# Fill products behind the state product, heads in turn, and a read in four parts in a two-layer hybrid mixer

## The chip, the core and the metric
The program runs on one core of one Trainium2 chip. Time is the device time of one execution in microseconds (us). The engines are named as in the profile: PE is TensorE (PEld its weight loads), DVE VectorE, ACT ScalarE, POOL GpSimd, SP SyncE, which issues the DMAs here.

## What is computed
Two layers on 512 tokens of width 1024, all in float32. Each layer is a SwiGLU block, a mixer with three branches, and a second SwiGLU block, each added to the stream behind an RMS norm. The branches are a retention (8 heads, chunks of 128 tokens), an attention over the 256 keys that an index score selects, and RWKV-7. The change lies in RWKV-7 and in the retention. RWKV-7 is, per head of 64, a recurrence over the tokens:

```
def step(S, inp):
    r_t, w_t, k_t, v_t, kk_t, a_t = inp
    sa = jnp.einsum('bhvk,bhk->bhv', S, -kk_t)
    S = S * w_t[:, :, None, :] + sa[..., None] * (kk_t * a_t)[:, :, None, :] + v_t[..., None] * k_t[:, :, None, :]
    return S, jnp.einsum('bhvk,bhk->bhv', S, r_t)
```

The retention computes within each chunk `scores = jnp.einsum('bhid,bhjd->bhij', qc, kc) * decay_mask` and multiplies them with the values.

## The kernel before, in words
Everything lies feature by token, in tiles of 128 partitions by 512 tokens. The large products (SwiGLU, all projections, the merge) are run as three float32r products each of a high and a low part (lines 109, 111, 113, `mm3`); the split of every weight tile costs ScalarE one copy (L49) and VectorE one subtraction (L50), and its load comes by SyncE (L54) into one of four `raw` buffers.

RWKV-7 is computed in 8 chunks of 64 tokens, for two heads at a time: a head pair p = 0 to 3 fills the 128 partitions, head 0 on rows 0 to 63, head 1 on rows 64 to 127. A pair passes through four stages. `front2` makes decays, keys and stacked operands. `mid` multiplies `bk` by `st` for each chunk and head (L444, a product over 64 rows: the head's), masks the result on VectorE into `nb`, `zo` and `st` (L449 to L451), transposes some operands, and then inverts a triangular matrix for each chunk: the 32x32 blocks of `nb` go to DRAM (four DMAs, L480, tile `dn`), come back as `N`, all 32 blocks side by side and repeated four times over the partitions (L481; the trace calls this tile by the name of its buffer, bk), and POOL solves row by row in 31 steps of two instructions (L490, L492, tile X, named cum in the trace). After every fourth step a one-column product, the pace product (L494), makes TensorE wait for that step. The blocks of the inverse go to DRAM and back once more (L497, L503) and are put together (L504, L510, L517). `chain` then runs the 8 chunks one after the other: the product with the state (L533), a copy on VectorE (L536), the product with the inverse (L543), copies (L547), the state product (L553), the state update on VectorE (L556), and the output product (L558) with its sum Y (L562). L533, L543, L553 and L558 of a chunk write parts of one product buffer. `post` normalises.

Two product buffers (tag "r") serve mid, chain, front2 and post in turn; two (tag "f") serve retention and attention; four (tag "d") the dense products.

TensorE executes in one order, which a planner fixes at build time: it places instructions by level (the recurrence, "rec", first; fills, "norm", behind) as soon as its own clock has their operands ready. The other branches and the merge are a second stream of work. `K.fill(n, after)` takes n dense products from that stream, and ties them behind the instruction `after` on TensorE. The counts were written out by hand: FZ = 11 behind each group of L444, FV = 38 behind the transposes, FP = 11 to 15 behind each pace product, FD = 29 behind the last, and FC = 6, 6, 5, 6 (by head pair) three times in each chunk of the chain. `front2` of the next pair runs in steps within the chain of this one.

`Ret.heads` works on two heads as well: for each head four products over its 64 rows into one buffer (L673), then a mask on VectorE (L675). `kd` (L636, POOL) is the decayed key that L652 multiplies.

Of the kernel before, what the change touches and what calls it, by code (L numbers as in the profile page):

```python
# [7 lines left out]
P = 128  # L8
# [215 lines left out]
FZ, FV, FD, FB, FE = 11, 38, 29, 5, 46  # L224
FP = 12, 11, 11, 15
FM = 6, 0, 2, 7
FC = 6, 6, 5, 6
# [5 lines left out]
class Rwkv:  # L233
# [198 lines left out]
    def mid(self, d):  # L432

        nc, K, c = self.nc, self.K, self.cst
        st, bk, v = d["st"], d["bk"], d["v"]
        zo, nb = self.zo, self.t("kh", [P, 8, 64])
        for q in range(2):
            for h in range(2):
                s = slice(64 * h, 64 * h + 64)
                o = slice(64 - 64 * h, 128 - 64 * h)  # L440
                z = K.ps("r")
                for i in range(4):
                    ck = 4 * q + i
                    zl = nc.tensor.matmul(z[:, i * P:(i + 1) * P], bk[s, ck, :], st[h][s, ck, :], start=True, stop=True)  # L444
                K.fill(FZ, zl)
                z3 = z.rearrange("p (i t) -> p i t", i=4)
                mk = c["zmask"][:, h, None, :].to_broadcast([P, 4, P])
                cs = slice(4 * q, 4 * q + 4)
                nc.vector.tensor_tensor(out=nb[s, cs, :], in0=z3[s, :, s], in1=mk[s, :, s], op=ALU.mult)  # L449
                nc.vector.tensor_tensor(out=zo[s, cs, o], in0=z3[s, :, o], in1=mk[s, :, o], op=ALU.mult)  # L450
                nc.vector.tensor_tensor(out=st[h][o, cs, :], in0=z3[o], in1=mk[o], op=ALU.mult)  # L451
        with self.tc.issue_after(zl.ins):

            bt = d["bt"] = self.t("bkt", [P, 8, P])
            for q in range(2):
                pt = K.ps("r")
                for i in range(4):
                    K.turn(pt[:, i * P:(i + 1) * P], bk[:, 4 * q + i, :])
                nc.scalar.activation(bt[:, 4 * q:4 * q + 4, :], pt.rearrange("p (c t) -> p c t", c=4), AF.Copy)
            sv = d["sv"] = [self.t("sv0", [P, 8, 64]), self.t("sv1", [P, 8, 64])]  # L460
            pv = K.ps("r")
            for i in range(4):
                self.gate = K.turn(pv[:, i * P:(i + 1) * P], v[:, i * P:(i + 1) * P])
            pv4 = pv.rearrange("p (i h d) -> p i h d", i=4, h=2)
            for h in range(2):
                o = slice(64 - 64 * h, 128 - 64 * h)
                for par in range(2):
                    src = pv4[64 * par:64 * par + 64, :, h, :]
                    nc.scalar.activation(sv[h].rearrange("p (i e) d -> p i e d", e=2)[o, :, par, :], src, AF.Copy)
                nc.gpsimd.memset(sv[h][64 * h:64 * h + 64, 0, :], 0.0)  # L470
        if d["p"] < 3:
            K.urgent.append(self.front(d["p"] + 1, self.blk))
        K.fill(FV, self.gate)

        dn = K.dram([4, 8, 32, 32], "dn", 2)
        N = self.t("bk", [P, 32, 32])
        for h in range(2):
            for b in range(2):
                src = nb[64 * h + 32 * b:64 * h + 32 * b + 32, :, 32 * b:32 * b + 32]
                nc.sync.dma_start(dn[2 * h + b].rearrange("c s t -> s c t"), src)  # L480
        nc.sync.dma_start(N, dn.rearrange("b c s t -> (b c) s t")[None].to_broadcast([4, 32, 32, 32]))  # L481

        X = self.t("cum", [P, 8, 32])
        tmp = self.t("E", [P, 8 * 31])
        nc.sync.dma_start(X, c["idg"])
        FI, pz = FP[d["p"]], K.ps("r")
        for u in range(31):
            n, w = u // 4 + 1, 31 - u
            tv = tmp[:, :n * w].rearrange("p (s j) -> p s j", s=n)
            nc.gpsimd.tensor_tensor(out=tv, in0=X[:, 0:n, u:u + 1].to_broadcast([P, n, w]),  # L490
                                    in1=N[:, u:u + 1, u + 1:].to_broadcast([P, n, w]), op=ALU.mult)
            nc.gpsimd.tensor_tensor(out=X[:, 0:n, u + 1:], in0=X[:, 0:n, u + 1:], in1=tv, op=ALU.add)  # L492
            if FI and (u % 4 == 3 or u == 30):
                pace = nc.tensor.matmul(pz[:, u:u + 1], K.ident, X[:, 0, u + 1:u + 2], start=True, stop=True)  # L494
                K.fill(FI if u < 30 else FD, pace)
        dx = K.dram([4, 8, 32, 32], "dx", 2)
        nc.sync.dma_start(dx.rearrange("b c (i g) t -> g (b c) i t", g=4), X)  # L497
        mt = self.mt
        m1 = self.t("m1", [P, 8, 32])
        for h in range(2):  # L500
            a = 64 * h
            for b in range(2):
                nc.sync.dma_start(mt[a + 32 * b:a + 32 * b + 32, :, a + 32 * b:a + 32 * b + 32], dx[2 * h + b].rearrange("c s t -> s c t"))  # L503
            nc.vector.transpose(m1[a:a + 32].rearrange("p c t -> p (c t)"), mt[a:a + 32, :, a:a + 32])  # L504
            nc.gpsimd.memset(mt[a + 32:a + 64, :, a:a + 32], 0.0)
        pc = K.ps("r")
        cc = m1
        for a in (0, 64):
            for ck in range(8):
                mm = nc.tensor.matmul(pc[a + 32:a + 64, ck * 32:ck * 32 + 32], nb[a:a + 32, ck, 32:64], m1[a:a + 32, ck, :],  # L510
                                      start=True, stop=True)
        K.fill(2 * FB, mm)
        for a in (0, 64):
            nc.scalar.activation(cc[a + 32:a + 64], pc[a + 32:a + 64, :256].rearrange("p (c t) -> p c t", c=8), AF.Copy)
        for a in (0, 64):
            for ck in range(8):
                mm = nc.tensor.matmul(pc[a:a + 32, ck * 32:ck * 32 + 32], cc[a + 32:a + 64, ck, :], mt[a + 32:a + 64, ck, a + 32:a + 64],  # L517
                                      start=True, stop=True)
        K.fill(2 * FB, mm)
        for a in (0, 64):  # L520
            nc.scalar.activation(mt[a:a + 32, :, a + 32:a + 64], pc[a:a + 32, :256].rearrange("p (c t) -> p c t", c=8), AF.Copy)

    def chain(self, d, step):

        nc, K = self.nc, self.K
        st, bt, sv, gch = (d[x] for x in ("st", "bt", "sv", "gch"))
        Y = d["Y"] = self.t("Y", [P, 8, 64])
        half = lambda h: (slice(64 * h, 64 * h + 64), slice(64 - 64 * h, 128 - 64 * h))
        for ck in range(8):
            a = K.ps("r")  # L530
            a3 = a.rearrange("p (n h d) -> p n h d", n=4, h=2)
            for h in range(2):
                mm = nc.tensor.matmul(a3[:, 0, h, :], st[h][:, ck, :], sv[h][:, ck, :], start=True, stop=True)  # L533
# [5 lines left out]
            uvf = uv.rearrange("p h d -> p (h d)")  # L539
            for h in range(2):  # L540
                s, o = half(h)
                nc.gpsimd.tensor_copy(uv[o, h, :], sv[h][o, ck, :])
            mm = nc.tensor.matmul(a[:, 2 * P:3 * P], self.mt[:, ck, :], X, start=True, stop=True)  # L543
            K.fill(FC[d["p"]], mm)
            for h in range(2):
                s, o = half(h)
                nc.vector.tensor_copy(uv[s, h, :], a3[s, 2, h, :])  # L547
            if ck < 7:
                B = self.t("cb", [P, 64], bufs=2)
                for h in range(2):  # L550
                    s, o = half(h)
                    nc.vector.tensor_scalar(out=B[s], in0=sv[h][s, ck, :], scalar1=gch[s, ck:ck + 1], scalar2=None, op0=ALU.mult)
                nc.tensor.matmul(a[:, P:2 * P], bt[:, ck, :], uvf, start=True, stop=True)  # L553
                for h in range(2):
                    s, o = half(h)
                    nc.vector.scalar_tensor_tensor(out=sv[h][s, ck + 1, :], in0=a3[s, 1, h, :], scalar=gch[s, ck:ck + 1], in1=B[s],  # L556
                                                   op0=ALU.mult, op1=ALU.add)
            mm = nc.tensor.matmul(a[:, 3 * P:], self.zo[:, ck, :], uvf, start=True, stop=True)  # L558
            K.fill(FC[d["p"]] if ck < 7 else FE, mm)
            for h in range(2):  # L560
                s, o = half(h)
                nc.vector.tensor_tensor(out=Y[o, ck, :], in0=a3[o, 3, h, :], in1=X[o, s], op=ALU.add)  # L562
# [38 lines left out]
class Ret:  # L601
# [43 lines left out]
    def heads(self, q, X, kd):  # L645
        K, nc, c = self.K, self.nc, self.c

        pk = K.ps()
        for j in range(3):
            for h in range(2):  # L650
                s = slice(64 * h, 64 * h + 64)
# [8 lines left out]
        for o, dst in ((0, qT), (P, kT)):  # L660
            pt = K.ps()
            for t in range(4):
# [1 line left out]
            nc.scalar.activation(dst, pt, AF.Copy)  # L664
        nc.gpsimd.tensor_tensor(out=qd.rearrange("p (c i) -> p c i", c=4), in0=qT.rearrange("p (c i) -> p c i", c=4),
                                in1=self.qdec[:, None, :].to_broadcast([P, 4, P]), op=ALU.mult)
        sT = []
        for h in range(2):
            s = slice(64 * h, 64 * h + 64)
            pt = K.ps()  # L670
            for j in range(4):
                f = slice(j * P, j * P + P)
                last = nc.tensor.matmul(pt[:, f], kT[s, f], qT[s, f], start=True, stop=True)  # L673
            x = self.t("sT", bufs=2)
            nc.vector.tensor_tensor(out=x.rearrange("p (c i) -> p c i", c=4), in0=pt.rearrange("p (c i) -> p c i", c=4),  # L675
                                    in1=self.dm[:, h:h + 1, :].to_broadcast([P, 4, P]), op=ALU.mult)
            sT.append(x)
# [480 lines left out]
```

## Time and profile before

| | |
|---|---|
| median of three runs | 3042.56 us (3041.69 to 3042.8) |
| the profiled execution | 3045.66 us, of which its span 3043.9 us |
| TensorE matmuls busy | 2908.3 us (96%) |
| VectorE busy | 1741.9 us (57%) |
| ScalarE busy | 1082.4 us (36%) |
| POOL busy | 736.7 us (24%) |
| mean granted clock of TensorE | 0.982 |
| the chain that ended last | PE 73%, DVE 10%, POOL 7%, DMA 6% |

A float32 product of small tiles shows as two records (a count of x8 is four products). Matmul records overlap, so the distance from start to start tells more than their length. A wait in the list of waits is idle time of the engine, put down to what ended it.

### The profile page before, as it was taken

The page shows a single profiled execution, that of the slowest core. Times are in us where ns is not written, and L with a number is a line of the kernel's source. Part 1 is how long each engine was busy: PE and PEld are TensorE (multiplying, and loading weights), DVE is VectorE, ACT ScalarE, POOL GpSimd, SP SyncE. Part 2 cuts the span into 40 slices and gives each one's busy share as a digit, 9 for nine tenths or more (in the row PEclk, how much of TensorE's full clock was granted, in tenths as well). Part 3 has the DMA queues.
Part 4 walks back from the last instruction along what each step waited for, and adds up shares of the span by engine and source line. Part 5 has one row for each costly group of instructions (what it writes and reads, how often), then busy time and mean ns, then how long its engine had stood idle before and what let it go on. Part 6 is the DMA issues. An engine that isn't in the chain of part 4 may idle for free.

```text
span 3043.9 us, 39972 instructions
## 1 busy us (share of the span) xinstructions
PE 2908.3 (96%) x13968; PEld 2378.0 (78%) x13968; DVE 1741.9 (57%) x3694; ACT 1082.4 (36%) x1900; POOL 736.7 (24%) x1206
## 2 busy tenths in 40 slices
PE   9999999899899999999999999998988999999998
PEld 7888887777777778888888888777777777788886
DVE  5443378949674564444354433888485836644433
ACT  4333343244443233333333333533344432433322
POOL 2110124353433031110011101343534321311100
PEclk9999999999999999999999999999999999999999
DMA  4333322122324442333323334221323244423332
GB/s 137 97 97 104 112 92 73 63 88 81 94 84 148 131 153 94 97 97 95 100 94 97 97 107 118 83 71 60 95 74 97 92 143 132 145 94 97 97 97 87
DMA packets 198970, 305.66 MB, mean 100 GB/s; under 512 B 45808, under 2 KB 59888, under 8 KB 198768
## 3 DMA queue, kind: packets, MB, share of 16 engines
q1 hardware_dynamic: 198768, 303.10, 32.7%
q8 instruction: 110, 1.80, 0.3%
q14 instruction: 92, 0.75, 0.1%
HBM read 273.66 MB, written 29.36 MB: 100 GB/s over the span
## 4 chain that ended last, share of the span: by engine, by line
PE 73%; DVE 10%; POOL 7%; DMA 6%; issue 3%; ACT 1%; SPq 0%; DVEq 0%; POOLq 0%; ACTq 0%
PE psd L109 22%; PE psd L113 22%; PE psd L111 22%; POOL cum L492 3%; POOL E L490 2%; DMA bk<-dn 2%; DVE wlo L50 2%; DMA dx<-cum 1%; PE psr L444 1%; PE psr L533 1%; DMA th<-th 1%; PE psf L96 1%; DMA y<-y 1%; PE psr L558 1%; PE psr L96 1%
## 5 line engine op out<-in xcount | busy, mean ns | idle before, releaser
L49 ACT ACTIVATE whi<-raw 128x512 fp32r<-128x512 f32 (+2 forms) x920 | 571.3, 622 | 1300.8 <-PE psd L111 1002.6
L50 DVE TENSOR_TENSOR wlo<-raw,whi 128x512 fp32r<-128x512 f32 (+2 forms) x920 | 646.3, 703 | 552.7 <-ACT whi L49 545.4
L109 PE MATMUL psd<-xh,whi 128*128 128x512 f32 x2144 | 853.5, 398 | 1.5 <-DVE g L203 1.5
L111 PE MATMUL psd<-xl,whi 128*128 128x512 f32 x2144 | 848.9, 396 | 2.2 <-DVE xl L161 2.2
L113 PE MATMUL psd<-xh,wlo 128*128 128x512 f32 x2144 | 849.2, 396 | 0.1
L111 PEld LDWEIGHTS psd<-xl,whi 128*128 128x128 f32 x2144 | 408.1, 190 | 87.2 <-DVE xl L161 4.3
L113 PEld LDWEIGHTS psd<-xh,wlo 128*128 128x128 f32 x2144 | 408.0, 190 | 84.8 <-issue 0.7
L109 PEld LDWEIGHTS psd<-xh,whi 128*128 128x128 f32 x2144 | 408.5, 191 | 83.3 <-DVE g L203 1.7
L207 POOL TENSOR_TENSOR u<-s,u 128x512 f32<-128x512 f32 x88 | 140.9, 1602 | 841.6 <-DVE u L206 745.3
L109 PE MATMUL psd<-ah,whi 128*128 128x512 f32 x704 | 277.4, 394 | 0.0
L113 PE MATMUL psd<-ah,wlo 128*128 128x512 f32 x704 | 276.0, 392 | 0.0
L111 PE MATMUL psd<-al,whi 128*128 128x512 f32 x704 | 273.2, 388 | 0.0
L172 POOL TENSOR_TENSOR sq<-sq,sq 128x512 f32<-128x512 f32 x42 | 56.4, 1342 | 466.0 <-ACT sq L170 466.0
L111 PE MATMUL psd<-wlo,xh 128*128 128x512 f32 (+1 forms) x384 | 159.2, 415 | 0.0
L113 PEld LDWEIGHTS psd<-ah,wlo 128*128 128x128 f32 x704 | 132.1, 188 | 31.0
L111 PEld LDWEIGHTS psd<-al,whi 128*128 128x128 f32 x704 | 132.2, 188 | 29.6
L113 PE MATMUL psd<-whi,xl 128*128 128x512 f32 (+1 forms) x384 | 154.8, 404 | 0.0
L109 PEld LDWEIGHTS psd<-ah,whi 128*128 128x128 f32 x704 | 132.3, 188 | 26.3
L50 DVE TENSOR_TENSOR al<-u,ah 128x512 fp32r<-128x512 f32 x88 | 61.8, 702 | 153.6 <-ACT ah L49 153.6
L109 PE MATMUL psd<-whi,xh 128*128 128x512 f32 (+1 forms) x384 | 149.7, 410 | 0.0
L206 DVE TENSOR_TENSOR u<-psd,rb 128x512 f32<-128x512 f32 x88 | 60.9, 692 | 127.6 <-PE psd L113 127.6
L49 ACT ACTIVATE ah<-u 128x512 fp32r<-128x512 f32 x88 | 55.6, 632 | 169.4 <-POOL u L207 169.2
(305 smaller groups left out, 3946.6 us busy)
## 6 DMA issues: line engine op xcount, KB each, us to landing
raw<-in_wf_dram SPq DMA_DIRECT2D x184, 256.0 KB, 2.6
raw<-in_ffa_in_dram SPq DMA_DIRECT2D x176, 256.0 KB, 2.6
raw<-in_ffb_in_dram SPq DMA_DIRECT2D x176, 256.0 KB, 2.6
th<-th SPq DMA_DIRECT2D x96, 256.0 KB, 3.3
raw<-in_ffa_out_dram SPq DMA_DIRECT2D x80, 256.0 KB, 2.7
raw<-in_wt_dram SPq DMA_DIRECT2D x80, 256.0 KB, 2.8
raw<-in_ffb_out_dram SPq DMA_DIRECT2D x80, 256.0 KB, 2.6
x<-x SPq DMA_DIRECT2D x32, 256.0 KB, 4.4
```

The source lines that it names most:

```text
L49: self.nc.scalar.activation(hi, x, AF.Copy)
L50: self.nc.vector.tensor_tensor(out=lo, in0=x, in1=hi.bitcast(F32), op=ALU.subtract)
L96: return self.nc.tensor.transpose(out, x, self.ident)
L109: nc.tensor.matmul(out, ah, bh, start=start, stop=False)
L111: nc.tensor.matmul(out, ah, bl, start=False, stop=False)
L113: nc.tensor.matmul(out, al, bh, start=False, stop=stop)
L172: nc.gpsimd.tensor_tensor(out=sq, in0=sq, in1=self.ssq[0], op=ALU.add)
L206: nc.vector.tensor_tensor(out=u, in0=pu, in1=self.rb, op=ALU.mult)
L207: nc.gpsimd.tensor_tensor(out=u, in0=s, in1=u, op=ALU.mult)
L444: zl = nc.tensor.matmul(z[:, i * P:(i + 1) * P], bk[s, ck, :], st[h][s, ck, :], start=True, stop=True)
L490: nc.gpsimd.tensor_tensor(out=tv, in0=X[:, 0:n, u:u + 1].to_broadcast([P, n, w]), in1=N[:, u:u + 1, u + 1:].to_broadcast([P, n, w]), op=AL ...
L492: nc.gpsimd.tensor_tensor(out=X[:, 0:n, u + 1:], in0=X[:, 0:n, u + 1:], in1=tv, op=ALU.add)
```

## The change
Three places. In `chain` the fill that stood behind the output product L558 of the chunks 0 to 6 stands behind the state product L553; the last chunk keeps its fill FE. In `mid` the products of both heads are issued in turn into two buffers, with one fill of 2 x FZ behind both instead of FZ behind each, and then the masks of both heads; `heads` does the same with L673, without fills. In `mid` the read of `N` is issued as four DMAs of eight rows each instead of one.

```diff
         for q in range(2):
+            zz = [K.ps("r") for _ in range(2)]
+            for i in range(4):
+                ck = 4 * q + i
+                for h in range(2):
+                    s = slice(64 * h, 64 * h + 64)
+                    zl = nc.tensor.matmul(zz[h][:, i * P:(i + 1) * P], bk[s, ck, :], st[h][s, ck, :], start=True, stop=True)
+            K.fill(2 * FZ, zl)
             for h in range(2):
                 s = slice(64 * h, 64 * h + 64)
                 o = slice(64 - 64 * h, 128 - 64 * h)
-                z = K.ps("r")
-                for i in range(4):
-                    ck = 4 * q + i
-                    zl = nc.tensor.matmul(z[:, i * P:(i + 1) * P], bk[s, ck, :], st[h][s, ck, :], start=True, stop=True)
-                K.fill(FZ, zl)
-                z3 = z.rearrange("p (i t) -> p i t", i=4)
+                z3 = zz[h].rearrange("p (i t) -> p i t", i=4)
...
-        nc.sync.dma_start(N, dn.rearrange("b c s t -> (b c) s t")[None].to_broadcast([4, 32, 32, 32]))
+        for u in range(0, 32, 8):
+            src = dn.rearrange("b c s t -> (b c) s t")[:, u:u + 8, :]
+            nc.sync.dma_start(N[:, u:u + 8, :], src[None].to_broadcast([4, 32, 8, 32]))
...
-                nc.tensor.matmul(a[:, P:2 * P], bt[:, ck, :], uvf, start=True, stop=True)
+                mm = nc.tensor.matmul(a[:, P:2 * P], bt[:, ck, :], uvf, start=True, stop=True)
                 for h in range(2):
                     s, o = half(h)
                     nc.vector.scalar_tensor_tensor(out=sv[h][s, ck + 1, :], in0=a3[s, 1, h, :], scalar=gch[s, ck:ck + 1], in1=B[s],
                                                    op0=ALU.mult, op1=ALU.add)
+                K.fill(FC[d["p"]], mm)
             mm = nc.tensor.matmul(a[:, 3 * P:], self.zo[:, ck, :], uvf, start=True, stop=True)
-            K.fill(FC[d["p"]] if ck < 7 else FE, mm)
+            if ck == 7:
+                K.fill(FE, mm)
...
-        sT = []
-        for h in range(2):
-            s = slice(64 * h, 64 * h + 64)
-            pt = K.ps()
-            for j in range(4):
-                f = slice(j * P, j * P + P)
-                last = nc.tensor.matmul(pt[:, f], kT[s, f], qT[s, f], start=True, stop=True)
+        sT, ps = [], [K.ps() for _ in range(2)]
+        for j in range(4):
+            f = slice(j * P, j * P + P)
+            for h in range(2):
+                s = slice(64 * h, 64 * h + 64)
+                last = nc.tensor.matmul(ps[h][:, f], kT[s, f], qT[s, f], start=True, stop=True)
+        for h, pt in enumerate(ps):
             x = self.t("sT", bufs=2)
```

## Rows read from the trace of the kernel before

**Rows 1.** The page, busy time of each engine (us, share of the span, instructions).
```profile
PE 2908.3 (96%) x13968; PEld 2378.0 (78%) x13968; DVE 1741.9 (57%) x3694; ACT 1082.4 (36%) x1900; POOL 736.7 (24%) x1206
```

**Rows 2.** Who waited for whom, TensorE over the whole span: us in total, times, longest us.
```profile
PE psr L494 <- POOL cum L492: 24.8, 20, 5.7
PE psr L533 <- DVE sv L556: 17.8, 24, 1.8
PE psr L510 <- DVE m L504: 12.0, 14, 2.4
...
PE psf L652 <- POOL kd L636: 7.1, 4, 3.3
PE psr L553 <- DVE uv L547: 6.1, 8, 1.6
...
PE psr L558 <- DVE sv L556: 3.8, 4, 1.3
```

**Rows 3.** Timeline of TensorE in a chunk of the last head pair's chain, first layer: start, length, line, operation, tiles, shapes, count, idle time before.
```profile
1008.92 0.38 PE L553 MATMUL psr<-uv,bkt 128*128 128x128 f32 x2
1009.68 0.43 PE L533 MATMUL psr<-sv,stk 128*128 128x64 f32 x2 [0.37 <-DVE sv L556]
1010.00 0.49 PE L558 MATMUL psr<-uv,zo 128*128 128x128 f32 x2
1010.32 0.33 PE L533 MATMUL psr<-sv,stk 128*128 128x64 f32 x2
...
1010.78 0.39 PE L111 MATMUL psd<-yl,whi 128*128 128x512 f32 x1
...
1013.32 0.39 PE L543 MATMUL psr<-cx,mt 128*128 128x128 f32 x2
...
1014.95 0.38 PE L553 MATMUL psr<-uv,bkt 128*128 128x128 f32 x2
```

**Rows 4.** Timeline of VectorE in the same chunk.
```profile
1009.35 0.60 DVE L556 SCALAR_TENSOR_TENSOR sv<-psr,gch,cb 64x64 f32<-64x64 f32 x2 [0.89 <-PE psr L553]
...
1010.91 0.27 DVE L536 COPY cx<-psr 128x128 f32<-128x128 f32 x1
```

**Rows 5.** Busy time by stretch: the chains of the first, third and fourth head pair of the first layer. Columns: stretch, its length, then busy us and instructions of PE, PEld, DVE, ACT, POOL, then the granted clock, the DMA share and GB/s.
```profile
512.00:600.00 88.00, 77.86 (x444) 62.17 (x442) 82.54 (x224) 28.37 (x50) 31.98 (x50) 0.94 0.23 71
...
850.00:914.00 64.00, 57.34 (x314) 46.70 (x313) 54.05 (x155) 27.10 (x54) 25.33 (x29) 1.00 0.25 78
...
990.00:1046.00 56.00, 52.98 (x263) 43.91 (x262) 29.94 (x87) 10.76 (x17) 2.81 (x12) 1.00 0.39 123
```

**Rows 6.** Timeline of TensorE around products of 64 rows, of 64 columns and of full size, from three stretches.
```profile
447.06 0.39 PE L111 MATMUL psd<-wlo,xh 128*128 128x512 f32 x1
...
447.38 1.16 PE L444 MATMUL psr<-stk,bk 64*128 64x128 f32 x8
...
448.80 0.39 PE L109 MATMUL psd<-whi,xh 128*128 128x512 f32 x1
...
470.49 0.66 PE L652 MATMUL psf<-X,kd 128*64 128x128 f32 x8
...
498.55 0.60 PE L686 MATMUL psf<-X,sT 128*128 128x128 f32 x4
...
771.38 1.71 PE L444 MATMUL psr<-stk,bk 64*128 64x128 f32 x16
```

**Rows 7.** Timeline of TensorE, the retention's score products of one pair of heads.
```profile
491.89 1.16 PE L673 MATMUL psf<-qT,kT 64*128 64x128 f32 x10
...
493.43 0.93 PE L673 MATMUL psf<-qT,kT 64*128 64x128 f32 x6
```

**Rows 8.** Timeline of TensorE at the end of the first head pair's chain: the next pair's first L444, and this pair's last L558.
```profile
598.80 1.16 PE L444 MATMUL psr<-stk,bk 64*128 64x128 f32 x8
...
604.00 0.49 PE L558 MATMUL psr<-uv,zo 128*128 128x128 f32 x2
```

**Rows 9.** Timeline of VectorE there.
```profile
601.51 0.41 DVE L450 TENSOR_TENSOR zo<-psr,zmask 64x256 f32<-64x256 f32 x1
...
604.53 0.46 DVE L562 TENSOR_TENSOR Y<-psr,cx 64x64 f32<-64x64 f32 x2
```

**Rows 10.** Timeline of POOL, the first step of the first inversion loop.
```profile
474.72 0.24 POOL L490 TENSOR_TENSOR E<-cum,bk 128x31 f32<-128x31 f32 x1 [7.05 <-DMA bk<-dn]
```

**Rows 11.** The chain that ended last, in order of time: start, length, what.
```profile
463.96 10.62 DMA bk<-dn
```

**Rows 12.** Timeline of TensorE behind two pauses (first head pair; third head pair).
```profile
476.51 0.70 PE L652 MATMUL psf<-X,kd 128*64 128x128 f32 x4 [3.25 <-POOL kd L636]
...
477.73 0.63 PE L111 MATMUL psd<-wlo,xh 128*128 128x512 f32 x1
478.16 0.63 PE L113 MATMUL psd<-whi,xl 128*128 128x512 f32 x1
...
802.42 0.38 PE L494 MATMUL psr<-cum,ident 128*128 128x1 f32 x2 [4.69 <-POOL cum L492]
```

**Rows 13.** Busy time by stretch, a microsecond while the N of the fourth head pair is read (columns as in rows 5).
```profile
936.00:937.00 1.00, 1.00 (x6) 0.75 (x6) 0.00 (x0) 0.01 (x1) 0.00 (x0) 1.00 0.26 86
```

**Rows 14.** DMA issues: tiles, engine, count, KB each, median us from issue to landing.
```profile
cum<-in_idg_dram SPq DMA_DIRECT2D x8, 128.0 KB, 2.0
```

**Rows 15.** Line 481 by itself: count, duration of the issue on SyncE in ns (min/median/max), first and last start.
```profile
L481 SPq DMA_DIRECT2D bk<-dn x8: 541/542/678, 464.0 to 2443.8; - x8
```

## Prediction
> **What bounds the kernel now.** I read the page first: TensorE's matmuls are busy 95.5% of the span, VectorE's instructions 57% [rows 1]. The kernel is one long row of dense products, and what can be won is the time in which TensorE stands still or runs products badly packed. Second, the list of who waited for whom, TensorE alone [rows 2]: the largest entries are the three the change touches. The pace products (L494) wait 24.8 us for POOL's inversion loop, the state products (L533) 17.8 us for VectorE's state update (L556), the blocks of the inverse (L510) 12.0 us for what comes after that loop; L652 waits 7.1 us for kd (L636), which stands on POOL behind the loop's first step. Third, the timeline of one chunk of the chain [rows 3, 4]; fourth, the timelines of the 64-row products [rows 6, 7]; last, the transfer that the loop starts on [rows 10 to 15].
>
> **Part A, the third fill of the chain.** A chunk from one L553 to the next takes 1014.95 - 1008.92 = 6.03 us [rows 3]. Its work: 18 fill products at 0.23 us from start to start (the second of twelve starts at 1010.78, L543 behind the last at 1013.32: eleven steps), 4.1 us; ten records of small products at about 0.1 us, 1.0 us; together 5.1 us. So 0.9 us is lost, and the rows say where: L553 starts at 1008.92, needs 0.22 us, and the first L533 starts at 1009.68, because VectorE's L556 runs from 1009.35 to 1009.95 [rows 4]. L558 then stands between the two L533 and each waits a little (starts 0.32 us apart instead of about 0.2). Nothing is queued on TensorE that could stand in this gap, since the fill is tied behind L558, and L558 writes the product buffer that L556 reads (its own wait for L556 is 3.8 us [rows 2]). Behind the gap twelve fills follow in a row (2.8 us) where the copy of L536, which L543 needs, ends at 1011.18 [rows 4], 0.9 us after the second L533 started.
> After the change six fills (1.4 us) stand in the gap, which needs 1009.95 - 1009.14 = 0.8 us of cover; six stay before L543, which needs about 0.9 us. No fill is added or dropped. Expected loss per chunk: about 0.15 us; gain 0.75 us where VectorE is free. Chunks with a state product: 7 x 8 pairs = 56. The four head pairs of a layer differ by VectorE's load: 53% in the last one's chain, 94% in the first's and 84% in the third's [rows 5], and I take the second to lie between; there a reply of VectorE comes late whatever TensorE does, and six fills will not always cover it. The nearest row for such a reply behind six fills is L553 waiting for L547: 6.1 us in 8 waits [rows 2]. Last head pairs: 14 x 0.75 = 10 us. The others: 42 x 0.35 (about half) = 15 us. A = **25 us**. Bounds: the waits of L533 and L558 alone, 21.6, less two stretches like L553's 6.1, gives 9; all 56 at 0.75 gives 42. New waits: L558 and the Y sums (L562) come 1.4 us later and hold their product buffer that much longer; the buffer's ring has two, so this matters only while the other is taken (rival 3).
>
> **Part B, products of L444.** A batch of eight records takes from 447.06 (the fill before) to 448.80 (second fill after), 1.74 us, where two fill steps take 0.46: 1.28 us, of which eight records at 0.11 are 0.9 us and 0.4 us are the change of shape before and after [rows 6]. Whether rows 0-63 and rows 64-127 run beside each other has two rows of this trace. Two batches that happen to be neighbours take 1.71 us for 16 records, not twice 1.16 [rows 6]. And L652, which alternates halves of the columns, brings eight records in 0.66 us where four of L686 take 0.60 [rows 6]. So I take both heads in turn at the time of one batch: 1.28 us for 16 records. There are 16 such couples of batches (two a head pair). In the first head pair of each layer they stand apart (4 couples): 1.28 us each, 5 us. In the other 12 they are partly neighbours already, or the first head's batch runs inside the previous chain and its partner must wait for the second ring buffer [rows 8]; 0.25 us each, 3 us. B = **8 us**, bounds 3 and 16.
> The Trainium skill (TensorE: Matmul & The Clock Gate, Part 3) has products in strict order in start and end; by that rule neighbouring batches could not have gained anything and B would be nearer 16. The 1.71 us of this trace disagree: some of the overlap is there already.
> The 22 fills now stand in one block behind both heads, 5.1 us, where eleven (2.5 us) covered three of VectorE's instructions each time; they now cover six, and nothing is charged. If VectorE is late there, the next couple waits for both buffers.
>
> **Part D, products of L673.** Eight uses; four have a pace product in the middle (1.16 + 0.93 us) [rows 7], four are 16 neighbours. At 1.28 each they save 1 us and 0.4 us: 5.6 us if all are laid as meant; half the split ones will be split again by a pace product that has precedence. D = **4 us**, bounds 0 and 6.
>
> **Part C, four parts of N.** POOL waits 7.05 us until 474.72 [rows 10], for a transfer that took 10.6 us [rows 11], and everything behind it on POOL waits too, kd among it (TensorE idles 3.25 us for it before 476.51 [rows 12]). While it runs, the transfers keep 0.26 of 16 engines busy [rows 13], about four. A quarter has 128 KB; the load of idg, of that size, lands in 2.0 us [rows 14]. A quarter of the 10.6 less 2.0, and 2.0: about 4.2 us; so L490 can start up to 6 us earlier, if it waits for its own eight rows alone. That it can: L450 wrote chunks 0 to 3 of zo at 601.51 while L558 had yet to read chunk 7 of that tile at 604.00 [rows 8, 9], so dependencies go by region. The loop's first eight rows are two of its stretches, with 11 to 15 fills beside each (2.5 us and more), and the parts follow each other by about 2.2 us, so the later ones are hidden. SyncE issues three more transfers of 0.54 us [rows 15]; the weight loads queued behind them come 1.6 us later, which four raw buffers cover; without them a late load would cost TensorE at most that, 8 x 1.6 = 13 us.
> What the 6 us are worth: at most the waits that hang on the loop, 24.8 + 12.0 + 7.1 = 43.9 us [rows 2]. TensorE however reaches the first pace product earlier too, by B, and past some point its own queue is the bound. I take the long waits of the first pace products, such as the 4.69 us before 802.42 [rows 12], at 14 us of the 24.8, and half of L652's 7.1: C = **18 us**. Bounds: 5 (the one longest kind of wait, once in each layer) and 44.
>
> **The clock.** In the mixers the granted clock falls: its mean is 0.94 over the first chain and 1.00 over the third and fourth [rows 5]. It is 1.2 GHz in parts of the first: after the 3.25 us of idling, fills start 0.43 us apart [rows 12], not 0.23. Over the chain of 88 us 0.06 is 5 us. Idle stretches that go take some of this with them: **5 us** in all, bounds 0 and 25.
>
> **Sum.** 25 + 8 + 4 + 18 + 5 = 60 us. The profiled execution took 3045.66 us (span 3043.9, 1.8 around it), 3.1 us over the median of 3042.56. 3045.7 - 60 = 2985.7, less 3.1: **2983 us**. Under 0.2% (6 us) a measurement cannot tell a change of this kernel.
>
> **Rivals.** 1. VectorE becomes the bound of the first three chains (84 to 94% busy): A keeps the last pairs' 10 us, C half, no clock: 10 + 8 + 4 + 9 = 31 us, 3012. For it: the load [rows 5]; against it: part of that load is top-k work that has no haste.
> 2. All waits go and the clock stays up: 42 + 10 + 5 + 25 + 13 = 95 us, 2948. For it: the idle time is short and scattered, so a little cover reaches far.
> 3. Slower: the ring of two product buffers. L558 and Y late, the front work of the next pair in the other buffer, so the next L533 has to wait for Y: about 1.1 us (L558 0.2, Y 0.9) in up to 30 chunks, 33 us; and at 6 ends of chains the second head's batch waits, from 598.80 to Y's end at 604.99 [rows 8, 9], which strips TensorE of a batch and 11 fills of cover, 3.7 us each, 22 us. Against it 16 (26 free chunks at 0.6) + 3 + 4 + 18 = 41 us: 14 us slower, 3057. It decides from stalls of 41 us on. Against it: now, too, Y comes only after L533's wait, and front products leave their buffer within about a microsecond.
> 4. The four parts do not do what they should: L490 waits for the last, which is issued 1.6 us later than the one of now. C is 0 to -13 us (1.6 x 8): 3001 to 3014, I say 3003. The Trainium skill has a rule on its side: DMA: Bandwidth & Descriptors (Bandwidth) wants at least 1 MiB in a transfer, and by its fit (Anatomy of one DMA, for transfers that GpSimd issues) of 2.0 us plus the bytes over 436 GB/s a whole N would be an estimated 3.2 us and a quarter 2.3, so that C would be 7 us and the time 2994. The 10.6 us of this trace disagree with that fit.
>
> **How the numbers follow.** Forecast 0.42; rival 1 0.24; rival 2 0.14; rival 3 0.04; rival 4 0.12; no change that can be told, by gains and stalls that cancel, 0.04. Faster 0.92, same 0.04, slower 0.04. Range: 2948 to 3022: rivals 1, 2 and 4 lie in it; above it are rival 3, no change and the tail of 1.
>
> **What will show it.** A: fills between L553 and L533, and L533's wait for L556 under 8 us. B, D: 16 records in about 1.2 us. C: L490 starting 4 to 5 us after the first part's issue, L494's waits under 8 us. Wrong if L533 now waits for L562, if L543 waits for L536 by over 10 us, or if POOL still waits 10 us.

## The result, and the profile after

The changed kernel takes 3000.66 us (median of four, 3000.12 to 3009.55), the kernel before 3042.68 beside it: ratio 0.9855, 95% interval 0.9835 to 0.9876. That is 42 us less by the medians and 44 by the ratio (38 to 50), where 60 were forecast; 3000.7 lies within 2948 to 3022. The profiled execution took 3000.62 us, its span 2998.8. Its mean granted clock is 0.986, where the kernel before had 0.982; in the three other runs of the changed kernel it is 0.983.

TensorE's list of waits, by columns as in rows 2. Lines have moved: L494 is now L498, L533 L537, L510 L514, L652 L658, L553 L557, L558 L563, L543 L547, L562 L568, L444 L443, L490 L494, L673 L678.

```profile
PE psr L498 <- POOL cum L496: 14.8, 23, 1.6
PE psr L514 <- DVE m L508: 12.2, 12, 2.2
PE psf L96 <- POOL o L706: 8.6, 4, 4.2
PE psr L390 <- DVE Y L568: 8.2, 6, 1.9
...
PE psr L537 <- DVE sv L560: 5.3, 3, 2.8
...
PE psr L443 <- DVE Y L568: 5.0, 5, 2.6
...
PE psr L284 <- DVE Y L568: 3.6, 4, 1.5
```

Against [rows 2] the pace products wait 14.8 us instead of 24.8, and no longer than 1.6 at a time instead of 5.7; the products with the state (L537) 5.3 instead of 17.8; L658's 7.1 are gone from the top. The blocks of the inverse wait as before (12.2 and 12.0). Three lines tell of Y: 8.2 + 5.0 + 3.6 = 16.8 us in which TensorE, at first products of other work (L390 and L284 in the front work, L443 the 64-row products), waits for a product buffer until the Y sums have read it. In the kernel before, L284 alone had such a wait, 1.2 us.

A chunk of the last head pair's chain, first layer, TensorE and then VectorE (columns as in rows 3 and 4):

```profile
995.88 0.38 PE L557 MATMUL psr<-uv,bkt 128*128 128x128 f32 x2
996.02 0.48 PE L109 MATMUL psd<-yh,whi 128*128 128x512 f32 x1
...
997.50 0.33 PE L537 MATMUL psr<-sv,stk 128*128 128x64 f32 x2
997.66 0.44 PE L563 MATMUL psr<-uv,zo 128*128 128x128 f32 x2
997.94 0.33 PE L537 MATMUL psr<-sv,stk 128*128 128x64 f32 x2
998.08 0.48 PE L109 MATMUL psd<-yh,whi 128*128 128x512 f32 x1
...
999.56 0.38 PE L547 MATMUL psr<-cx,mt 128*128 128x128 f32 x2
...
1001.17 0.38 PE L557 MATMUL psr<-uv,bkt 128*128 128x128 f32 x2
```
```profile
996.30 0.60 DVE L560 SCALAR_TENSOR_TENSOR sv<-psr,gch,cb 64x64 f32<-64x64 f32 x2 [0.90 <-PE psr L557]
...
998.22 0.46 DVE L568 TENSOR_TENSOR Y<-psr,cx 64x64 f32<-64x64 f32 x2
998.60 0.27 DVE L540 COPY cx<-psr 128x128 f32<-128x128 f32 x1
```

It takes 1001.17 - 995.88 = 5.29 us, 0.74 less than [rows 3]. Fills stand from 996.02 on; the state update ends at 996.90, 0.6 us before L537 wants it.

The 64-row products, in two stretches (columns as in rows 6):

```profile
447.06 1.16 PE L443 MATMUL psr<-stk,bk 64*128 64x128 f32 x8
448.14 0.45 PE L759 MATMUL psf<-kih,qs 128*128 128x384 f32 x1
448.43 0.34 PE L760 MATMUL psf<-X,qs 128*128 128x384 f32 x1
448.69 1.16 PE L443 MATMUL psr<-stk,bk 64*128 64x128 f32 x8
...
612.81 1.16 PE L443 MATMUL psr<-stk,bk 64*128 64x128 f32 x16
613.90 0.50 PE L113 MATMUL psd<-whi,xl 128*128 128x512 f32 x1
```

Where the heads really alternate, 16 records take the 1.16 us of eight [rows 6]. But only 6 of the 16 couples (the two heads' batches of one stretch of four chunks) came out so. In the other ten the planner issued the first head's four products as soon as they were ready, and other work stands between the heads.

POOL's first step of the inversion, and the four reads by themselves (columns as in rows 10 and 15):

```profile
468.33 0.24 POOL L494 TENSOR_TENSOR E<-cum,bk 128x31 f32<-128x31 f32 x1 [3.28 <-DMA bk<-dn]
```
```profile
L485 SPq DMA_DIRECT2D bk<-dn x32: 499/510/725, 464.0 to 2408.1; - x32
```

The first quarter is issued at 464.0 and POOL starts at 468.33, 4.3 us later, where the whole took 10.6 us to land [rows 10, 11]. Over the eight head pairs it is 4.1 to 6.7 us, the longest in the fourth pairs; in the kernel before, 9.4 to 12.0.

### The profile page after: what moved, and what is told of

The parts are those of the page before. It is cut to its first block, busy times and chain, and to the rows that moved or that the text cites. A ratio compares the mean times of both kernels' runs of the same rounds, so it can differ in the third digit from the quotient of the medians.

```text
span 2998.8 us, 39997 instructions
## 1 busy us (share of the span) xinstructions
PE 2884.7 (96%) x13968; PEld 2356.4 (79%) x13968; DVE 1751.9 (58%) x3694; ACT 1081.0 (36%) x1900; POOL 739.9 (25%) x1206
```

## The experiments

All are timed beside the kernel before. First each part alone: a_only, b_only, c_only and d_only hold the diff's hunk for `chain`, for L444, for the read of N and for L673, and nothing else.

**a_only.**
```diff
+                K.fill(FC[d["p"]], mm)
...
-            K.fill(FC[d["p"]] if ck < 7 else FE, mm)
+            if ck == 7:
+                K.fill(FE, mm)
```


> The kernel before with part A alone (third fill behind the state product). As predicted, A is worth 25 us: 3018 us. The theory that A works only in the last head pair's chain, where VectorE is half idle and no front work of a next pair uses the product buffers, expects its two chains to be 5 us shorter each and the other six unchanged within 3 us: about 3030 us, and waits of front products for Y in the list of waits, as in the changed kernel (16 us there).

Measured 3036.42 us, 0.9976 (0.9966 to 0.9986): 7 us, not 25. TensorE's waits:

```profile
PE psr L494 <- POOL cum L492: 25.3, 16, 5.2
PE psr L510 <- DVE m L504: 16.5, 14, 2.3
PE psr L96 <- DVE bc L396: 15.5, 4, 5.5
PE psf L654 <- POOL kd L638: 12.9, 4, 3.8
```

The 17.8 us of L533 are gone from the top, so A does its work; others have grown. The eight chains, each from the start of its first L533 to that of its last L558, sum to 581.7 us (590.8 before), the mids in front of them, from the first 64-row product on, to 643.3 (634.6): of 9.1 us won 8.7 are given back there. The last pairs' chains are 5.6 us shorter each, as the second theory says, and its waits for Y are there (7.7 + 3.7 + 2.9 us); the time is 6 us over its 3030. What is given back lies in the mids of the fourth head pairs, 7.2 and 4.3 us longer (the other six together 2.8 shorter), and only there does the read of N land more than a microsecond later. In the first layer POOL starts 13.5 us after the issue at 933.38, where before it took 9.3 (933.47 to 942.81), in the second 14.0 instead of 10.2:

```profile
946.87 0.24 POOL L490 TENSOR_TENSOR E<-cum,bk 128x31 f32<-128x31 f32 x1 [9.36 <-DMA bk<-dn]
```

Busy time by stretch while N is read, the kernel before and then a_only (columns as in rows 5; the DMA share is the last but one):

```profile
936.00:938.00 2.00, 2.00 (x12) 1.66 (x12) 0.82 (x2) 0.96 (x2) 0.00 (x0) 1.00 0.37 113
938.00:940.00 2.00, 2.00 (x11) 1.61 (x10) 0.47 (x1) 1.71 (x5) 0.00 (x0) 1.00 0.62 176
```
```profile
936.00:938.00 2.00, 2.00 (x12) 1.67 (x10) 1.22 (x2) 1.88 (x6) 0.57 (x2) 1.00 1.02 253
938.00:940.00 2.00, 2.00 (x10) 1.65 (x9) 0.37 (x1) 1.17 (x3) 0.00 (x0) 1.00 1.06 217
...
944.00:946.00 2.00, 0.99 (x5) 0.49 (x3) 0.00 (x0) 0.00 (x0) 0.00 (x0) 1.00 0.63 157
946.00:948.00 2.00, 0.00 (x0) 0.00 (x0) 0.00 (x0) 0.00 (x0) 1.03 (x5) 0.79 0.40 155
```

Other transfers fill the DMA engines (share 1.0 instead of 0.4 to 0.6) while N crosses, and TensorE, out of covering work, stands from 945 to 948. In the second layer the share is 0.83 over the read. That the other transfers make N late is read from these shares, not tested by itself. The clock has a part as well: over the twelve runs of a_only its mean is 0.978, over the kernel before's beside them 0.982.

**b_only** (the hunk for L444, with the fill of 2 x FZ).

> The kernel before with part B alone (64-row products of mid, both heads in turn, one fill of 22 behind them). As predicted 8 us: 3035 us, most of it in the first head pair of each layer. The theory that B's worth is mostly in the earlier start of the inversion (eleven fills fewer ahead of the last product) expects more, 3025 to 3030 us, with the pace products' waits for POOL below 20 us instead of 24.8. The theory that the second product buffer is missed at the ends of the chains expects 3040 us or more.

Measured 3045.59 us, 1.001 (0.9999 to 1.0021): nothing, or up to 0.2% lost. That is the time of the third theory, but waits of the 64-row products for Y, which it implies, are not in the list.

**c_only** (the read of N in four DMAs).

> The kernel before with part C alone (N read in four parts). As predicted 18 us: 3025 us, the first step of the loop 4 to 7 us behind the first issue instead of 10.6, the pace products' waits under 12 us, the blocks' wait (L510) unchanged near 12 us. If the page rule against small transfers were right, 7 us: 3036 us. If what is gained ahead of the loop is given back behind it, 3035 us or more, with L510 waiting over 16 us.

Measured 3023.37 us, 0.9931 (0.9917 to 0.9945): 21 us. TensorE's waits:

```profile
PE psr L535 <- DVE sv L558: 22.4, 24, 3.3
...
PE psr L496 <- POOL cum L494: 8.8, 14, 1.1
```

The pace products wait 8.8 us instead of 24.8, and POOL's first step comes 3.8 to 5.3 us after the first issue in all eight head pairs. The products with the state (here L535) wait 22.4 us; in b_only and d_only it is 23.8 and 25.0, so that the growth from 17.8 is not C's alone.

**d_only** (both heads in turn in L673).

> The kernel before with part D alone (the retention's score products, both heads in turn). As predicted 4 us: 3039 us. The rival, that the planner's new order costs what the overlap saves, expects 3041 to 3045 us, and the score products' batches still cut by pace products.

Measured 3043.54 us, 0.9996 (0.9985 to 1.0007): no difference. Four of the eight uses are 16 records in 1.16 us, the other four are still cut by a pace product.

**ac**: both together, without B and D.

> The kernel before with parts A and C. Alone they measured ratios of 0.9976 and 0.9931, together by multiplication 0.9907 (3014 us); the whole change has 0.9855. Theory that what A wins in the chains is given back at the inversion's read of N and is kept only where C shortens that read: 3000 to 3006 us (ratio 0.986 to 0.988). Theory that the missing part is B's doing: 3012 to 3016 us.

Measured 3001.31 us, 0.9849 (0.9833 to 0.9865): the whole change. Against c_only, A on top of C is 0.9849/0.9931 = 0.9917, 25 us (19 to 32 by the two intervals); alone it was 7. The chains by head pair, c_only and ac, both layers:

| head pair | 1 | 2 | 3 | 4 |
|---|---|---|---|---|
| c_only, us | 95.8, 94.9 | 82.0, 82.0 | 67.3, 67.5 | 57.6, 57.6 |
| ac, us | 97.4, 96.6 | 81.5, 76.1 | 65.4, 63.4 | 50.5, 50.6 |

The chains are 23 us shorter: 14.1 in the last pairs, 6.0 in the third, 6.4 in the second, and 3.3 longer in the first. But a length also counts the fills and front products that the planner put into the chain. The last pair's, first layer, c_only and then ac (columns as in rows 5):

```profile
978.10:1036.00 57.90, 54.88 (x270) 45.48 (x269) 30.90 (x89) 12.01 (x19) 2.85 (x12) 1.00 0.39 120
```
```profile
975.00:1025.80 50.80, 50.80 (x261) 42.81 (x260) 29.77 (x87) 10.76 (x17) 3.20 (x12) 1.00 0.43 135
```

c_only's chain has nine products more, 2.1 us at 0.23 us each; the other 5.0 us are A's. Counted in this way in all eight chains (an estimate, with 0.23 us for a product of 512 columns and 0.11 for a record of a small one), A brings 10 us in the last pairs, 7 in the third, and in the second and first nothing that can be told: 18 us. What is left of the 25 lies outside the chains.

**bc**: B and C.

> The kernel before with parts B and C. By multiplication 0.9941 (3025 us). Theory that the read of N hides what A wins: 3022 to 3027 us, B adds nothing here. Theory that B's tighter products pay once the loop no longer holds TensorE up: 3010 to 3015 us.

Measured 3024.1 us, 0.9925 (0.991 to 0.994), with C alone 0.9931: B brings nothing with the wait for N out of the way either.

**tied**: the whole change, and each 64-row product tied behind the one before, so that one head's products can't run ahead of the other's; head 1 now comes first.
```diff
+            zl = None
             for i in range(4):
                 ck = 4 * q + i
-                for h in range(2):
+                for h in (1, 0):
                     s = slice(64 * h, 64 * h + 64)
-                    zl = nc.tensor.matmul(...)
+                    with ExitStack() as es:
+                        if zl:
+                            es.enter_context(self.tc.issue_after(zl.ins))
+                        zl = nc.tensor.matmul(...)
```


> The whole change, with each 64-row product of the mids tied behind the one before it, heads in turn, so that the two heads' products come alternately wherever both buffers are there. In the changed kernel 10 of the 16 couples still stood apart as two batches of eight. Theory 1 (B gave nothing because the order of the build split the couples): ten couples at 1.28 us less each than two batches, up to 10 us: 2988 to 2995 us, and batches of 14 to 16 records. Theory 2 (a batch's price is not on the path, because the time is made up at the next wait for VectorE or POOL or for the second product buffer): 2997 to 3004 us. Theory 3 (the first head's products now wait for the second head's buffer, and TensorE with them): over 3004 us.

Measured 3009.8 us, 0.9892 (0.9878 to 0.9906): 11 us slower than the changed kernel by the ratios. TensorE at the first couple of the second head pair, L447 being the 64-row products:

```profile
604.39 0.48 PE L447 MATMUL psr<-stk,bk 64*128 64x128 f32 x2
...
610.01 1.16 PE L447 MATMUL psr<-stk,bk 64*128 64x128 f32 x14
```

In 12 of the 16 couples the planner still splits off one product, and the other seven follow as 14 records in 1.16 us; the first pairs' four couples come whole. But here the 14 come at 610 us, and the masks run on VectorE from 612.9. In the changed kernel the first head's eight come at 602.1, inside the previous chain, and its masks run from 604.03. From a chain's end to the next pair's first pace product, in the first layer, it is now 31.9, 33.4 and 31.9 us instead of 22.7, 26.1 and 27.2. Only the first pair, whose couples were split with both buffers free, reaches it sooner (26.9 us from its first 64-row product instead of 29.3). Part of that is work moved: the eight chains are 36 us shorter in all, as the early batch and its fills no longer stand in them. So theory 1 falls: the couples packed cost 11 us more, and theory 3 fits the place. That the early half batch was worth more than the packing is argued from these times; the tie also cut six couples that had been whole.

**zofirst**: the output product ahead of the state product in the chunks 0 to 6, the fill behind both.
```diff
             if ck < 7:
                 ...
+                nc.tensor.matmul(a[:, 3 * P:], self.zo[:, ck, :], uvf, start=True, stop=True)
                 mm = nc.tensor.matmul(a[:, P:2 * P], bt[:, ck, :], uvf, start=True, stop=True)
                 ...
                 K.fill(FC[d["p"]], mm)
-            mm = nc.tensor.matmul(a[:, 3 * P:], self.zo[:, ck, :], uvf, start=True, stop=True)
             if ck == 7:
+                mm = nc.tensor.matmul(a[:, 3 * P:], self.zo[:, ck, :], uvf, start=True, stop=True)
                 K.fill(FE, mm)
```


> The changed kernel with the output product ahead of the state product in chunks 0 to 6, the fill behind both. Ring theory (Y comes late behind the fill, holds one of two product buffers, and front products and 64-row products wait for it, 16.8 us in the changed kernel): these waits for Y fall under 5 us, the chains of the first three head pairs shorten by 2 to 4 us each, 2985 to 2993 us. VectorE theory (84 to 94% busy in those chains): waits move to other instructions, time within 4 us of the changed kernel. Price: the state product comes 0.22 us later in 56 chunks, behind six fills that cover it.

Measured 2996.64 us, 0.9834 (0.982 to 0.9849); ac on the same chip 3001.31. Its waits:

```profile
PE psr L498 <- POOL cum L496: 14.9, 26, 1.5
PE psf L96 <- POOL o L707: 14.4, 4, 6.8
PE psr L514 <- DVE m L508: 11.9, 8, 2.5
PE psr L537 <- DVE sv L561: 11.9, 12, 3.4
```

The waits for Y are gone: the late output product did hold the ring's buffers. But L537 waits 11.9 us instead of 5.3 and L96 14.4 instead of 8.6: of 16.8 us some 5 are kept, a difference that the interval of the changed kernel (0.9835 to 0.9876) and this one's do not tell from nothing.

**fd40**: FV 27 instead of 38 and FD 40 instead of 29, so 11 fills move from behind the transposes to the end of the inversion loop, to cover L514.
```diff
-FZ, FV, FD, FB, FE = 11, 38, 29, 5, 46
+FZ, FV, FD, FB, FE = 11, 27, 40, 5, 46
```


> The changed kernel with FV 27 and FD 40 in place of 38 and 29: eleven fills moved from ahead of the inversion loop to behind it. Theory that C left a slack ahead of the loop and a wait behind it (the blocks' product waits 12.2 us in the changed kernel): that wait falls under 4 us, 2990 to 2996 us. Theory that the fills are missed ahead of the loop: the pace products wait over 20 us for POOL instead of 14.8, 3000 us or more.

Measured 2994.84 us, 0.983 (0.9815 to 0.9846), some 6 us if it is a difference (the intervals overlap); and not by the cover: L514 still waits 13.4 us, and only 13 to 20 fills stand between the last pace product and L514 in the second to fourth pairs of either kernel (31 to 33 in the first), since the planner's clock places L514 ahead of the rest. Where the 6 us come from is open.

**zo_fd40**: the two together.

> The changed kernel with both small gains together: the output product ahead of the state product in the chunks 0 to 6 with the fill behind both (4 us alone), and 11 of the 38 fills behind the transposes moved to the end of the inversion loop (6 us alone). If the two act at different places, the sum: 2990 us, 2988 to 2993. If both only move the same waits about, 2994 to 2997.

Measured 2986.09 us, 0.981 (0.9796 to 0.9823): they add up, and the two together are clear of the changed kernel's interval. It is the fastest of the kernels that compute the whole, 14 us (0.5%) under the changed kernel.

**before_top1** and **after_top1**: the kernel before and the changed one, with fifteen of the sixteen turns of the attention's top-k loop left out (VectorE's work).
```diff
-                for _ in range(16):
+                for _ in range(1):
```


> The kernel before with one turn of the top-k loop in the place of sixteen (VectorE work left out). It is the base for the changed kernel with the same cut. VectorE is 94% busy in the first chain, so if that load costs time at all this is faster than the kernel before by 10 to 30 us; if top-k is hidden everywhere, within 6 us of it.

> The changed kernel with one turn of the top-k loop in the place of sixteen, so that the attention's keys are chosen by the first eight values alone: this leaves work out, on VectorE alone, and most of that in the chains of the first head pairs. To be read against the kernel before with the same cut. If VectorE holds back part of A in the first three chains, the change is worth more here than the 42 us that it is worth with the whole loop: the remaining 17 us of the forecast come, 55 to 60 us between the two. If the load of VectorE is not what limits A, the difference stays at 38 to 46 us.

Measured 3015.54 us, 0.9915 (0.9902 to 0.9928), and 2969.76 us, 0.9758 (0.9745 to 0.9771). So those turns cost 28 us in the kernel before; but the change is worth 3015.5 - 2969.8 = 46 us without them and 42 with them, a difference that the intervals do not tell from nothing. Without top-k the missing 18 us do not come. But the cut relieves VectorE in the first pair's chain only; the first and the second pair's in before_top1 (columns as in rows 5):

```profile
517.90:587.80 69.90, 67.67 (x406) 54.56 (x404) 54.47 (x144) 24.03 (x43) 25.88 (x41) 1.00 0.24 73
672.50:747.80 75.30, 68.05 (x354) 55.95 (x353) 69.08 (x218) 35.41 (x82) 29.91 (x41) 0.95 0.28 82
```

In the first, VectorE is busy 54.5 of 69.9 us (94% in [rows 5]) and TensorE idle 2.2 us, so that A finds next to nothing to fill; in the second VectorE is still 92% busy. So these runs do not tell whether VectorE holds A back there. In after_top1 TensorE still waits for Y:

```profile
PE psr L284 <- DVE Y L568: 3.9, 4, 1.6
PE psr L390 <- DVE Y L568: 3.7, 2, 1.9
```

## Why the prediction came out as it did

**Direction and range were right; the forecast of 60 us was 18 too high.** Measured in the order C, A, B, D the parts are C 21, A 25, B 0 and D 0, together 46, where the whole is 42 to 44. A, C and the clock were forecast at 48 and came to 46, as the measured parts hold what the clock gave back. The step that failed is B's 8 and D's 4: they went into the sum as if time that TensorE saves on a batch were time off the end.

**A, 25 us: the mechanism right, the size met in part by luck.** Only behind C is it worth 25; alone it is 7, and C behind it then 39. I had summed parts of which one removes the wait that the other runs into. Alone, A's gain goes in the mids of the fourth pairs, where the read of N then lands 4 us later; in ac, where POOL needs the first quarter alone to start, its first step comes only 1.4 and 1.5 us later there than in c_only. That A needs C is measured; that the late N is the reason is read from the traces. By pairs, the last ones brought the forecast 10 us, the third 7, and the first two, where VectorE is 90 to 92% busy in ac, nothing that can be told; 15 were forecast for those six chains. What holds the first two is not settled: VectorE's load, which the top-k runs do not test there, and the new waits for Y are candidates. The forecast signs held: fills in the gap and L537 at 5.3 us, under 8; none of the signs of being wrong came (L547 waits 4.0 us for L540).

**C, 18 us: right, 21 measured.** POOL's first step starts 3.8 to 5.3 us after the issue in c_only, 4.2 being worked out, as it waits for its own eight rows alone; the pace products wait 8.8 us there. In the whole change they wait 14.8, above the 8 that I had named as its sign: with A in place TensorE presumably gets to them sooner. Rival 4 falls by c_only and these times, not by the total: its 3001 to 3014 begin where the measured time lies. The Trainium skill (DMA: Bandwidth & Descriptors, Anatomy of one DMA) would by its fit, which is for transfers that GpSimd issues, make a quarter an estimated 2.3 us and a whole N 3.2; the trace, where SyncE issues, shows 4.3 and 10.6, so the split was worth three times the 7 us of that rival. The whole read kept about four of 16 engines busy [rows 13]; whether a read spread over more of them would do without the split was not run.

**B, 8 us: mis-sized, nothing measured, and two steps behind it failed.** The price was right (16 records in 1.16 us). But I took the order of the text for the order on TensorE: the planner, which places by operands ready, split ten of sixteen couples, among them the four that were to bring 5 of the 8 us. Six couples came whole at 1.16 us, where six neighbours had taken 1.71: 3.3 us of batch time, which do not show at the end. And packing by force costs 11 us, presumably because an early first head's batch starts VectorE's masks inside the previous chain. In the forecast I had charged nothing for two heads waiting for each other.

**D, 4 us: mis-sized, nothing measured.** As feared, the pace product still has precedence:

```profile
486.90 0.71 PE L678 MATMUL psf<-qT,kT 64*128 64x128 f32 x8
488.37 0.38 PE L498 MATMUL psr<-cum,ident 128*128 128x1 f32 x2 [0.75 <-POOL cum L496]
488.68 0.71 PE L678 MATMUL psf<-qT,kT 64*128 64x128 f32 x8
```

In the changed kernel four of the eight uses are cut so, two are cut by L537, two are whole. The records lie ahead of waits for POOL like this one, so I read the lost gain as a longer wait there. In d_only's trace the pace products wait 27.6 us instead of 24.8; no run tests it further.

**The clock, 5 us: not told apart.** The mean went from 0.982 to 0.983 or 0.986, 0.1 to 0.4% of the span, so at most 3 to 12 us; no run separates it from the idle time that A and C remove. Busy time by stretch, the first and the fourth pair's chain of the changed kernel, first layer (columns as in rows 5):

```profile
509.70:607.20 97.50, 84.94 (x483) 67.20 (x480) 89.33 (x241) 30.97 (x54) 31.43 (x53) 0.91 0.21 66
...
977.30:1028.10 50.80, 50.80 (x261) 42.79 (x260) 29.76 (x87) 10.76 (x17) 3.21 (x12) 1.00 0.43 136
```

In the first chain, where I looked for it, the clock is 0.91 instead of 0.94 [rows 5], and VectorE is as busy as before; in the second layer's first chain it is 0.96 instead of 0.93. The fourth is now without a gap on TensorE, 50.80 of 50.80 us.

**The rivals.** Rival 4's time, 3003, lies nearest to 3000.7, and rival 1's 3012 nearer than the forecast's 2983. Rival 1 has C at half and A in the last pairs alone: C came whole, and the third pairs gave 7 us; that VectorE limits the first two pairs is left open. Rival 2 asked for all waits to go; 12 us stay at L514 and new ones came. Rival 3's mechanism is there in part: 16.8 us of waits for Y, all at first products of other work and hardly at L537, short of the 41 us from which it decides.

## What to carry over

Parts of a change are summed only after asking what each runs into: a stage that gets faster arrives earlier at the next transfer, and here A was worth 7 us or 25 by whether that transfer had been shortened. A part's worth then depends on the order in which the parts are taken, and a sum that comes near can hide it. A batch that gets shorter need not shorten the whole, as B and D show, and where a planner places instructions, the order in the program is a wish: read the order that came out. Before packing two products into one batch, look at whose work the earlier of them starts.

## What was not expected of the hardware

Alternating products on rows 0 to 63 and rows 64 to 127 overlap wholly (16 records in the 1.16 us of eight), while two batches that are merely neighbours took 1.71 [rows 6]. In the fourth head pair a read of 512 KB took 13.5 us instead of 9.3 from its issue to POOL's first step, with the DMA share at 1.0 instead of about 0.5 around it; a quarter of it took 4.1 to 6.7 us, well over a quarter of 10.6.
